# A one-core decoder layer: weight chunks taken in pairs, the later one first

## The chip, the core and the metric

The kernel runs on one core of a Trainium2 chip. The metric is the device time of one execution in microseconds (us); lower is better. Three runs of the kernel before gave a median of 2231.12 us (2229.8 to 2231.39).

## What is computed

One layer of a decoder on 256 tokens of width 2048, in float32: a gated feed-forward block (width 5504), a token mixer (two causal linear attentions, merged by gates), and a second feed-forward block, each with a norm before and one behind it.

```
f1 = swiglu(rms_norm(h, pre1), w_gate, w_up, w_down)      # (silu(x@w_gate) * (x@w_up)) @ w_down
h  = h + 0.5 * rms_norm(f1, post1)
m  = mixer(rms_norm(h, mix_pre))    # u@w_in, two attentions, gated sum of o@w_branch, then @w_out
h  = h + rms_norm(m, mix_post)
h  = h + 0.5 * rms_norm(swiglu(rms_norm(h, pre2), ...), post2)
```

## The kernel before

Every weight is read once from DRAM, in **chunks** of 128 x 1024 float32 values (512 KB). `wchunk` (L105) takes one chunk through three steps: SyncE issues a DMA into `raw` (L108), ScalarE rounds it into `whi` (L119), VectorE subtracts to get the rest, `wlo` (L120). A product is then three TensorE matmuls (`mm3`, L122): `xhi*whi` (L124), `xhi*wlo` (L125) and `xlo*whi` (L126), with the activations as the stationary operand and 512 columns of weights moving. One chunk feeds twelve such matmuls: two halves, times two token tiles, times three. `raw`, `whi` and `wlo` come from the pool `ring` with four buffers each, and each buffer is as large as the widest chunk of its tag, 2 x 528 values (4224 bytes a partition).

There are two loops over chunks. `gemm_block` (L128) makes 256 x 512 of `x @ W`: for each chunk of two k tiles it calls `mm` for token tile 0 and then 1, and then `side.pump()`, which lays one step of the small chains (transposes, attention levels) behind the twelve matmuls. It is used for the gate and up projections, for all of `w_in` and for the two branch weights. `out_proj` (L253) makes 256 x 2048 over all k tiles in eight accumulators; its chunks are one k tile by half of the columns (`hf`), in the table `order` (L278). At its first steps it also issues the products `early` on VectorE (L289), which need rows that `load_bcast` (L167) spreads over all partitions by DMA. Its last four k tiles (`tail`, L290) are used token tile by token tile; the `hf` 1 chunks of it lie in `held` buffers outside of the ring.

The order on each engine is the order of the code, as far as a scheduler keeps it: an instruction on ScalarE or VectorE that waits holds up what is behind it on that engine. At the end of a gate block ScalarE makes `silu` (L385) of both token tiles, at the end of an up block VectorE makes `hn` (L371); the down projection's left operand is split by L119 and L120 as well (`hkhi`, `hklo`). The lines that the loops consist of:

```
for k0 in range(0, nkt, 2):            # L149, gemm_block
    parts = chunk(k0, ring_alloc)
    for t in range(NT):
        mm(t, k0, parts)
    side.pump()
for i, (kt, hf) in enumerate(order):   # L280, out_proj
    parts = load(kt, hf)
    for t in range(NT):
        for n in (2 * hf, 2 * hf + 1):
            mm(t, n, kt, parts)
```

Of the kernel before, what the change touches and what calls it, by code (L numbers as in the profile page):

```python
# [16 lines left out]
D = 2048  # L17
NT = 2
# [13 lines left out]
class Side:  # L32
    """Chains of small steps whose instructions are laid between those of the large products.

    A light chain takes one step at every pump, the heavy ones take turns; a chain yields
    where the tensor engine would have to wait for what the other engines were just given."""

# [13 lines left out]
    def pump(self):  # L51
        for g in list(self.light):
            self._step(self.light, g)
        if self.heavy:
            g = self.heavy.pop(0)
            # two at a time take turns
            self.heavy.insert(min(1, len(self.heavy)), g)
            self._step(self.heavy, g)
# [12 lines left out]
def kernel(ctx: ExitStack, tc: tile.TileContext, a: dict, out: bass.AP):  # L71
# [26 lines left out]

    # ------------------------------------------------------------------ weights
    def ring_alloc(w):  # L100
# [4 lines left out]
    def wchunk(src: bass.AP, w: int, alloc=ring_alloc):  # L105
        """src: [128, 2, w] of a weight in DRAM -> the float32r parts (hi, lo) of its two halves."""
        raw = ring.tile([P, 2, w], F32, tag="raw", name=nm("raw"))
        nc.sync.dma_start(raw, src)  # L108
        parts = alloc(w)
        if len(parts) == 1:  # L110
            split_into(*parts[0], raw)
            hi, lo = parts[0]
            return [(hi[:, i, :], lo[:, i, :]) for i in range(2)]
        for i, (hi, lo) in enumerate(parts):
            split_into(hi, lo, raw[:, i, :])
        return parts
# [11 lines left out]
    def gemm_block(w_dram, c0, w, lhs, nkt=KT, held=None):  # L128
        """[256, w] of x @ W, one bank a token tile (two halves in two banks if w > 512). With
        held, the chunks after the ring's stay in its tiles, and token tile 1 comes after all  # L130
        of token tile 0."""
        nb = -(-w // CB)
        pss = [[ps_tile(f"mm{t}") for _ in range(nb)] for t in range(NT)]

        def chunk(k0, alloc):
            return wchunk(w_dram[k0 * P:(k0 + 2) * P, c0:c0 + w].rearrange("(k p) c -> p k c", p=P),
                          w, alloc)

        def mm(t, k0, parts):
            for i, part in enumerate(parts):  # L140
                kt = k0 + i
                x = lhs(t, kt)
                for j, ps in enumerate(pss[t]):
                    sl = slice(j * (w // nb), (j + 1) * (w // nb))
                    mm3(ps[:, :w // nb], x, (part[0][:, sl], part[1][:, sl]),
                        kt == 0, kt == nkt - 1)

        if held is None:
            for k0 in range(0, nkt, 2):  # L149
                parts = chunk(k0, ring_alloc)  # L150
                for t in range(NT):
                    mm(t, k0, parts)
                side.pump()
        else:
            kept = []
            for i, k0 in enumerate(range(0, nkt, 2)):
                kept.append((k0, chunk(k0, ring_alloc if i < 4 else held)))
                mm(0, *kept[-1])
                side.pump()
            for k in kept:  # L160
                mm(1, *k)
                side.pump()
            side.flush()
        return pss if nb > 1 else [ps[0] for ps in pss]

    # ------------------------------------------------------------------ helpers
    def load_bcast(name, after):  # L167
        """A row of 2048 on every partition, in four tiles; not before `after` is issued."""
        ts = []
# [7 lines left out]
    def rstd(ss, n, width, tag):  # L177
        """(ss / n + eps) ** -0.5 for ss [128, width]."""
        v = small.tile([P, width], F32, tag=f"{tag}v", name=nm("v"))
# [17 lines left out]
    def lhs_of(x):  # L197
        def lhs(t, kt):
            # the products are laid behind the transposes that they read
            side.until(lambda: x[2][t] > kt)  # L200
            return x[0][t][:, kt, :], x[1][t][:, kt, :]
        return lhs

    def to_T(x, t, n, src):
        """src [128 tokens, 512] -> k tiles 4n.. of x's token tile t."""
        ps = ps_tile()
# [5 lines left out]
    def rstd4(ss, scale, tag):  # L212
        """rstd of rows of D whose squares' sums are in the four columns of ss; all but the
        last column is added up beforehand. scale: a power of two, into the result."""
        c = 1.0 / (D * scale * scale)
# [14 lines left out]
    def first_norm(t, x, rs, wcol):  # L230
        """x's token tile t = (h * w) transposed, the weights one channel a partition."""
        if t:
# [20 lines left out]
    def out_proj(w_dram, nkt, lhs, post, scale, pre, held, after):  # L253
        """acc = lhs @ W [256, 2048]; h += scale * rmsnorm(acc) * post; then the next
        sublayer's transposed operand (h * pre, and the rows' rstd, applied later), or the
        kernel's output."""
        acc = [[None] * 4 for _ in range(NT)]
        wpost = load_bcast(post, after)
        early, nxt, rs = [], None, [None, None]
        if pre is not None:  # L260
            # h * pre + rstd * acc * (post * pre): all but the second product ahead of time
            wpre = load_bcast(pre, after)
# [17 lines left out]
        for i, (kt, hf) in enumerate(order):  # L280
            parts = load(kt, hf)
            for t in range(NT):
                for n in (2 * hf, 2 * hf + 1):
                    mm(t, n, kt, parts)
            if i == 1:
# [12 lines left out]
        def finish(t, ss):  # L298
# [6 lines left out]
            if pre is None:  # L305
                # GpSimd takes one of the four
                for n in range(4):
# [46 lines left out]

    # ------------------------------------------------------------------ FFN
    def ffn(pre, x, rs, post, pre_next):
# [49 lines left out]

    # ------------------------------------------------------------------ mixer
    def mixer(x, rs):
        xl = lhs_of(x)
        w_in = a["w_in"]  # L410
        with ExitStack() as mctx:
# [11 lines left out]

            # masks of the small levels' pairs, four heads wide, and of the diagonal
            diag = mp.tile([P, P], U8, name="diag")
# [8 lines left out]

            # lower bounds of the HGRN forget gates: softmax over the two rows of logits,
            # one head a column
            lg = blk("lg")
# [34 lines left out]
            def transposed(src, dst):  # L472
                """A step later, dst = src with each 128 columns transposed."""
                yield
# [21 lines left out]
            def spawn_T(srcs, s):  # L496
                """Transposes of the two token tiles' blocks, a step later."""
                dsts = []
# [5 lines left out]
            def attention(t, qT, kT, fT, vs, gates, dv, br, b0):  # L504
                """Four heads of 128 key channels on token tile t; fT: the decays. kT holds
                each key times the decays after it in its block, qT each query times those up
                to it; from level to level the blocks double, and the pairs of a block's halves
                get their scores, as products of two factors in [0, 1]."""
                sc = blk("sc")
# [11 lines left out]
                for lv, c in enumerate(LEVELS):  # L521
# [11 lines left out]
                    else:  # L533
                        # the blocks' rectangles lie on the engine's own borders
                        for r0 in range(0, P, 2 * c):
# [99 lines left out]
            def gla_decays(code, fT):  # L635
                """exp(logsigmoid(code @ w + b) / 16), transposed; logsigmoid(y) as
                min(y, 0) - ln(1 + exp(-|y|))."""
                cs = blk("code")
# [38 lines left out]
            def hgrn_gates(y, t, g, fT, kT):  # L677
                """f = lb + (1 - lb) sigmoid(y) and 1 - f = (1 - lb) sigmoid(-y), transposed."""
                yield
# [11 lines left out]

            # ---- GLA
            qT = spawn_T([scaled(q[t], rq[t], "q") for t in range(NT)], "qT")
            # the 16 columns of the gate's code, and beside them the first 512 of h_q
            fT, hqs = [blk("fT") for _ in range(NT)], [blk("hq") for _ in range(NT)]
# [19 lines left out]

            # ---- HGRN2, four heads at a time
            for g in range(2):
# [15 lines left out]

            # ---- gated merge
            ms = []
# [24 lines left out]

    # ------------------------------------------------------------------ the layer
    warm = const.tile([P, 1], F32, name="warm")
# [60 lines left out]
```

## Time and profile before

| | us |
|---|---|
| median of three runs | 2231.12 |
| span of the profiled execution, first to last instruction | 2230.0 |
| its own time, span and what lies around it | about 2231.1, by the median |
| TensorE matmul busy (PE) | 2203.5 |
| VectorE busy (DVE) | 1183.0 |
| ScalarE busy (ACT) | 995.1 |
| HBM read, mean | 183 GB/s over the span |

The profile names no time of the profiled execution beside its span; the median lies 1.1 us above the span, and that is taken as what lies around it. PE is the matmul, PEld the weight load that goes ahead of it on TensorE, and SP the queue that issues the weights' DMAs. Matmul durations overlap, so the pace of TensorE is read from the starts of the weight loads, of which each matmul has one: a matmul starts about when the load behind its own starts.

### The profile page before, as it was taken

What the parts mean: (1) busy time and instruction counts of PE and PEld (TensorE: products, weight loads), DVE (VectorE), ACT (ScalarE), POOL (GpSimd) and SP (SyncE); (2) the same over time, 40 slices, a digit from 0 to 9 for tenths busy, and PEclk for the clock granted to TensorE, in tenths of its full rate; (3) what the DMA queues carried; (4) which work ended last, traced back from release to release, by engine and by line L of the source; (5) the groups of instructions that cost most, each with busy time, mean ns of one, the idle gap of its engine ahead of it and who ended that gap; (6) DMA issues with size and microseconds to landing.
All of it is one profiled execution on the core that took longest, in us unless ns stands there. A gap on an engine that the chain in (4) does not pass through costs nothing.

```text
span 2230.0 us, 26331 instructions
## 1 busy us (share of the span) xinstructions
PE 2203.5 (99%) x10197; PEld 1816.2 (81%) x10197; DVE 1183.0 (53%) x1278; ACT 995.1 (45%) x1202; POOL 69.1 (3%) x106
## 2 busy tenths in 40 slices
PE   8999999999999999999999999999999999999998
PEld 6888888898888788888888888878888888898886
DVE  5544444446555744657575656465444444445554
ACT  5444444444444564444434444355444444444443
POOL 0000000000000400000000000021000000000001
PEclk9999999999999999999999999999999999999999
DMA  7666666666666556655556775555666666666664
GB/s 233 186 187 185 189 186 185 189 200 205 190 192 196 159 171 189 170 148 145 155 154 174 232 204 185 183 171 177 188 189 186 184 188 189 170 217 190 191 193 135
DMA packets 189344, 410.24 MB, mean 184 GB/s; under 512 B 13681, under 2 KB 22289, under 8 KB 189218
## 3 DMA queue, kind: packets, MB, share of 16 engines
q1 hardware_dynamic: 183712, 400.21, 60.6%
q10 hardware_dynamic: 5506, 8.34, 1.2%
q8 instruction: 80, 1.31, 0.2%
q14 instruction: 46, 0.38, 0.0%
HBM read 406.41 MB, written 2.10 MB: 183 GB/s over the span
## 4 chain that ended last, share of the span: by engine, by line
PE 64%; DVE 1%; POOL 1%; ACT 0%; issue 0%; DMA 0%; POOLq 0%; ACTq 0%
PE mm L124 16%; PE mm L126 16%; PE mm L125 16%; PE acc L125 5%; PE acc L126 5%; PE acc L124 5%; PE ps L187 1%; PE ps L531 1%; PE ps L581 0%; PE ps L538 0%; POOL h L303 0%; PE ps L515 0%; DVE tmp L295 0%; DMA raw<-in_ffn_w_down_dram 0%; POOL v L218 0%
## 5 line engine op out<-in xcount | busy, mean ns | idle before, releaser
L120 DVE TENSOR_TENSOR wlo<-raw,whi 128x1024 fp32r<-128x1024 f32 (+2 forms) x740 | 898.4, 1216 | 889.3 <-ACT whi L119 888.3
L119 ACT ACTIVATE whi<-raw 128x1024 fp32r<-128x1024 f32 (+2 forms) x740 | 777.1, 1051 | 1072.5 <-PE mm L126 800.5
L124 PE MATMUL mm<-whi,xhi 128*128 128x512 f32 (+2 forms) x2096 | 817.0, 390 | 3.6 <-ACT whi L119 3.6
L125 PE MATMUL mm<-wlo,xhi 128*128 128x512 f32 (+2 forms) x2096 | 809.6, 386 | 5.0 <-DVE wlo L120 5.0
L126 PE MATMUL mm<-whi,xlo 128*128 128x512 f32 (+2 forms) x2096 | 810.0, 386 | 0.0
L125 PEld LDWEIGHTS mm<-wlo,xhi 128*128 128x128 f32 x2096 | 394.7, 188 | 84.6 <-DVE wlo L120 6.2
L124 PEld LDWEIGHTS mm<-whi,xhi 128*128 128x128 f32 x2096 | 394.2, 188 | 83.0 <-ACT whi L119 4.0
L126 PEld LDWEIGHTS mm<-whi,xlo 128*128 128x128 f32 x2096 | 394.0, 188 | 81.1 <-DVE xlo L120 0.7
L125 PE MATMUL acc<-wlo,hkhi 128*128 128x512 f32 x656 | 257.6, 393 | 0.3 <-DVE wlo L120 0.3
L124 PE MATMUL acc<-whi,hkhi 128*128 128x512 f32 x656 | 257.2, 393 | 0.5 <-ACT hT L376 0.5
L126 PE MATMUL acc<-whi,hklo 128*128 128x512 f32 x656 | 257.5, 393 | 0.0
L125 PEld LDWEIGHTS acc<-wlo,hkhi 128*128 128x128 f32 x656 | 123.2, 188 | 29.2 <-DVE wlo L120 1.3
L124 PEld LDWEIGHTS acc<-whi,hkhi 128*128 128x128 f32 x656 | 123.2, 188 | 28.7 <-ACT hT L376 1.0
L126 PEld LDWEIGHTS acc<-whi,hklo 128*128 128x128 f32 x656 | 123.1, 188 | 27.7
L217 POOL TENSOR_TENSOR v<-ss 128x1 f32<-128x1 f32 x12 | 6.3, 524 | 1691.7 <-ACT sq L228 1690.8
L124 PE MATMUL mm<-whi,oT 128*128 128x512 f32 x128 | 51.3, 401 | 0.0
L126 PE MATMUL mm<-whi,oT 128*128 128x512 f32 x128 | 50.7, 396 | 0.0
L125 PE MATMUL mm<-wlo,oT 128*128 128x512 f32 x128 | 50.6, 395 | 0.0
L119 ACT ACTIVATE hkhi<-hT 128x512 fp32r<-128x512 f32 (+1 forms) x44 | 26.9, 621 | 52.2 <-PE acc L125 52.1
L120 DVE TENSOR_TENSOR hklo<-hT,hkhi 128x512 fp32r<-128x512 f32 (+1 forms) x44 | 29.6, 679 | 31.0 <-ACT hkhi L119 31.0
L125 PE MATMUL acc<-wlo,xhi 128*128 128x512 f32 x112 | 44.1, 394 | 0.0
L126 PE MATMUL acc<-whi,xlo 128*128 128x512 f32 x112 | 44.0, 393 | 0.0
(196 smaller groups left out, 1145.0 us busy)
## 6 DMA issues: line engine op xcount, KB each, us to landing
raw<-in_ffn_w_down_dram SPq DMA_DIRECT2D x172, 512.0 KB, 4.5
raw<-in_w_in_dram SPq DMA_DIRECT2D x168, 512.0 KB, 3.8
raw<-in_ffn_w_gate_dram SPq DMA_DIRECT2D x160, 512.0 KB, 3.8
raw<-in_ffn_w_up_dram SPq DMA_DIRECT2D x160, 512.0 KB, 3.6
raw<-in_w_out_dram SPq DMA_DIRECT2D x32, 512.0 KB, 4.1
raw<-in_w_branch_gla_dram SPq DMA_DIRECT2D x16, 512.0 KB, 3.6
raw<-in_w_branch_hgrn_dram SPq DMA_DIRECT2D x16, 512.0 KB, 3.8
raw<-in_ffn_w_gate_dram SPq DMA_DIRECT2D x16, 384.0 KB, 3.3
```

The lines of the kernel that those rows point to most:

```text
L119: nc.scalar.activation(hi, src, AF.Copy)
L120: nc.vector.tensor_tensor(lo, src, hi.bitcast(F32), op=ALU.subtract)
L124: nc.tensor.matmul(ps, lhsT=xhi, rhs=whi, start=start, stop=False)
L125: nc.tensor.matmul(ps, lhsT=xhi, rhs=wlo, start=False, stop=False)
L126: nc.tensor.matmul(ps, lhsT=xlo, rhs=whi, start=False, stop=stop)
L187: nc.tensor.transpose(dst_ps[:, i * P:(i + 1) * P], src[:, i * P:(i + 1) * P], ident)
L217: nc.gpsimd.tensor_tensor(v[:, 0:1], ss[:, 0:1], ss[:, 1:2], op=ALU.add)
L531: nc.tensor.matmul(ps[:, i * 64:(i + 1) * 64], lhsT=kT[:, sl], rhs=halves(qT[:, sl])[1], start=True, stop=True)
```

## The change

In `gemm_block`, two chunks are loaded together (A, then B), and each token tile takes four k tiles in the order B's first, A's first, A's second, B's second; `pump` follows each token tile, so again twelve matmuls. In `out_proj`, from the fifth chunk on, the chunks (kt, 0) and (kt, 1) are loaded together, and (kt, 1) is multiplied first. `held` blocks and the tail stay as they are. Comments were taken out too, so lines are about ten further down behind L290.

```
+        def one(t, kt, part, start, stop):
+            x = lhs(t, kt)
+            for j, ps in enumerate(pss[t]):
+                sl = slice(j * (w // nb), (j + 1) * (w // nb))
+                mm3(ps[:, :w // nb], x, (part[0][:, sl], part[1][:, sl]), start, stop)
...
-            for k0 in range(0, nkt, 2):
-                parts = chunk(k0, ring_alloc)
-                for t in range(NT):
-                    mm(t, k0, parts)
-                side.pump()
+            for k0 in range(0, nkt, 4):
+                parts = chunk(k0, ring_alloc) + chunk(k0 + 2, ring_alloc)
+                for t in range(NT):
+                    for i, o in enumerate((2, 0, 1, 3)):
+                        one(t, k0 + o, parts[o], k0 + i == 0, k0 + i == nkt - 1)
+                    side.pump()
...
-            parts = load(kt, hf)
-            for t in range(NT):
-                for n in (2 * hf, 2 * hf + 1):
-                    mm(t, n, kt, parts)
+            if i < 4:
+                use = [(hf, load(kt, hf))]
+            elif hf == 0:
+                use = [(0, load(kt, 0)), (1, load(kt, 1))][::-1]
+            else:
+                use = []
+            for j, parts in use:
+                for t in range(NT):
+                    for n in (2 * j, 2 * j + 1):
+                        mm(t, n, kt, parts)
```

TensorE in a gate block of the first feed-forward, before: the name's last number tells chunks apart, `Activation_49` counts ScalarE's instructions and `DVE_49` VectorE's. Token tile 0 writes `mm_213`, tile 1 `mm_214`.

```order
L124 MATMUL mm_213_1148<-whi_1218,xhi_2_99 128x512 [waits Activation_49]
L125 MATMUL mm_213_1148<-wlo_1219,xhi_2_99 128x512 [waits DVE_49]
L126 MATMUL mm_213_1148<-whi_1218,xlo_4_101 128x512
...
L124 MATMUL mm_214_1149<-whi_1218,xhi_3_100 128x512
...
L124 MATMUL mm_213_1148<-whi_1236,xhi_2_99 128x512 [waits Activation_49]
L125 MATMUL mm_213_1148<-wlo_1237,xhi_2_99 128x512 [waits DVE_49]
```

The same place now:

```order
L124 MATMUL mm_213_1148<-whi_1242,xhi_2_99 128x512 [waits Activation_49]
L125 MATMUL mm_213_1148<-wlo_1243,xhi_2_99 128x512 [waits DVE_49]
L126 MATMUL mm_213_1148<-whi_1242,xlo_4_101 128x512
L124 MATMUL mm_213_1148<-whi_1236,xhi_2_99 128x512
...
L124 MATMUL mm_213_1148<-whi_1242,xhi_2_99 128x512
...
L124 MATMUL mm_214_1149<-whi_1242,xhi_3_100 128x512
...
L124 MATMUL mm_214_1149<-whi_1236,xhi_3_100 128x512
...
L124 MATMUL mm_213_1148<-whi_1278,xhi_2_99 128x512 [waits Activation_49]
```

The two waits come every 24 matmuls instead of every 12, and the moving buffer changes after 3, 9, 15 and 21 of the 24. In the whole program TensorE's instructions that wait for ScalarE fall from 767 to 431.

ScalarE at the end of a gate block, before (the `silu` rows close the block, the `whi` rows are chunks of the next one):

```order
L119 ACTIVATE whi_1019<-raw_1017 128x1024 [waits DMAHW3_49,DVE_49,PE_49]
L119 ACTIVATE whi_1037<-raw_1035 128x1024 [waits DMAHW4_49,DVE_49,PE_49]
L385 ACTIVATE silu_993<-mm_154_835,r_201 128x512 [waits PE_49]
L385 ACTIVATE silu_995<-mm_155_836,r_305 128x512 [waits PE_49]
L119 ACTIVATE whi_1055<-raw_1053 128x1024 [waits DMAHW5_49,DVE_49]
```

and now:

```order
L119 ACTIVATE whi_1007<-raw_1005 128x1024 [waits DMAHW3_49,DVE_49,PE_49]
L395 ACTIVATE silu_993<-mm_154_835,r_201 128x512 [waits PE_49]
L119 ACTIVATE whi_1037<-raw_1035 128x1024 [waits DMAHW4_49,DVE_49,PE_49]
L395 ACTIVATE silu_995<-mm_155_836,r_305 128x512 [waits PE_49]
L119 ACTIVATE whi_1043<-raw_1041 128x1024 [waits DMAHW5_49,DVE_49]
```

Both `silu` still stand ahead of the second chunk of a pair, one of them now between the two chunks.

A third place is not moved, and the prediction reads the trace there: the tail of the last down projection, where each k tile's `held` chunk has its own two waits, three matmuls apart.

```order
L124 MATMUL acc_2869_14891<-held_16365,hkhi_16385 128x512 [waits Activation_49]
L125 MATMUL acc_2869_14891<-held_16366,hkhi_16385 128x512 [waits DVE_49]
L126 MATMUL acc_2869_14891<-held_16365,hklo_16386 128x512
L124 MATMUL acc_2869_14891<-held_16371,hkhi_16385 128x512 [waits Activation_49]
L125 MATMUL acc_2869_14891<-held_16372,hkhi_16385 128x512 [waits DVE_49]
L126 MATMUL acc_2869_14891<-held_16371,hklo_16386 128x512
L124 MATMUL acc_2869_14891<-held_16377,hkhi_16395 128x512 [waits Activation_49]
L125 MATMUL acc_2869_14891<-held_16378,hkhi_16395 128x512 [waits DVE_49]
```

Only the names' numbers differ there after the change.

## Rows read from the trace of the kernel before

**Rows 1.** The page's head: span, busy time of each engine, instructions.
```profile
span 2230.0 us, 26331 instructions
...
PE 2203.5 (99%) x10197; PEld 1816.2 (81%) x10197; DVE 1183.0 (53%) x1278; ACT 995.1 (45%) x1202; POOL 69.1 (3%) x106
...
PEclk9999999999999999999999999999999999999999
```

**Rows 2.** Waits of TensorE: who for whom, us in total, times, longest.
```profile
PE mm L125 <- DVE wlo L120: 5.0, 3, 2.0
...
PE mm L124 <- ACT whi L119: 3.6, 1, 3.6
PE acc L125 <- DVE held L120: 0.8, 1, 0.8
...
PE acc L125 <- DVE wlo L120: 0.3, 1, 0.3
```

**Rows 3.** Groups by shape: busy, mean ns of one | idle before, releasers.
```profile
L120 DVE TENSOR_TENSOR wlo<-raw,whi 128x1024 fp32r<-128x1024 f32 x700 | 857.9, 1227 | 844.7 <-ACT whi L119 844.0
...
L119 ACT ACTIVATE whi<-raw 128x1024 fp32r<-128x1024 f32 x700 | 741.5, 1060 | 1021.7 <-PE mm L126 753.4 <-PE acc L126 228.5 <-issue 13.8
...
L120 DVE TENSOR_TENSOR hklo<-hT,hkhi 128x512 fp32r<-128x512 f32 x42 | 28.7, 692 | 29.7 <-ACT hkhi L119 29.7
L371 DVE SCALAR_TENSOR_TENSOR hn<-mm,r,silu 128x512 f32<-128x512 f32 x40 | 28.3, 744 | 0.6 <-PE mm L126 0.6
L385 ACT ACTIVATE silu<-mm,r 128x512 f32<-128x512 f32 x40 | 27.6, 691 | 26.5 <-PE mm L126 23.4 <-POOL r L223 3.0
```

**Rows 4.** Timeline of weight loads, two chunks of a feed-forward block: start, us.
```profile
324.01 0.19 PEld L124 LDWEIGHTS mm<-whi,xhi 128*128 128x128 f32 x1
324.24 0.19 PEld L125 LDWEIGHTS mm<-wlo,xhi 128*128 128x128 f32 x1
...
324.93 0.19 PEld L125 LDWEIGHTS mm<-wlo,xhi 128*128 128x128 f32 x1
...
326.75 0.19 PEld L124 LDWEIGHTS mm<-whi,xhi 128*128 128x128 f32 x1
326.97 0.19 PEld L125 LDWEIGHTS mm<-wlo,xhi 128*128 128x128 f32 x1
...
329.76 0.19 PEld L125 LDWEIGHTS mm<-wlo,xhi 128*128 128x128 f32 x1
```

**Rows 5.** The same view, tail of the last down projection, waits every three.
```profile
2202.80 0.19 PEld L124 LDWEIGHTS acc<-held,hkhi 128*128 128x128 f32 x1
...
2204.16 0.19 PEld L124 LDWEIGHTS acc<-held,hkhi 128*128 128x128 f32 x1
```

**Rows 6.** The same view, same tail, another chunk every three, no waits.
```profile
2208.23 0.19 PEld L125 LDWEIGHTS acc<-wlo,hkhi 128*128 128x128 f32 x1
...
2213.09 0.19 PEld L125 LDWEIGHTS acc<-wlo,hkhi 128*128 128x128 f32 x1
```

**Rows 7.** Timeline of ACT, a feed-forward block: start, us, [idle before, releaser].
```profile
327.17 1.06 ACT L119 ACTIVATE whi<-raw 128x1024 fp32r<-128x1024 f32 x1 [1.67 <-PE mm L126]
```

**Rows 8.** Timeline of DVE behind it.
```profile
328.26 1.23 DVE L120 TENSOR_TENSOR wlo<-raw,whi 128x1024 fp32r<-128x1024 f32 x1 [1.51 <-ACT whi L119]
```

**Rows 9.** Timeline of ACT, start of the first down projection.
```profile
493.95 1.06 ACT L119 ACTIVATE whi<-raw 128x1024 fp32r<-128x1024 f32 x1 [1.77 <-DMA raw<-in_ffn_w_down_dram]
...
500.49 1.07 ACT L119 ACTIVATE whi<-raw 128x1024 fp32r<-128x1024 f32 x1 [1.20 <-DMA raw<-in_ffn_w_down_dram]
504.33 1.06 ACT L119 ACTIVATE whi<-raw 128x1024 fp32r<-128x1024 f32 x1 [2.77 <-DMA raw<-in_ffn_w_down_dram]
```

**Rows 10.** Timeline of DVE there: products ahead of time, beside the chunks.
```profile
506.37 1.29 DVE L289 TENSOR_TENSOR u<-h,row 128x512 f32<-128x512 f32 x2
507.57 1.22 DVE L120 TENSOR_TENSOR wlo<-raw,whi 128x1024 fp32r<-128x1024 f32 x1
```

**Rows 11.** The page's DMA issues: count, KB each, us to landing.
```profile
raw<-in_ffn_w_down_dram SPq DMA_DIRECT2D x172, 512.0 KB, 4.5
...
raw<-in_ffn_w_gate_dram SPq DMA_DIRECT2D x160, 512.0 KB, 3.8
```

More of the change, by code (lines that the diff above doesn't have):

```diff
@@ L137, in chunk @@
                           w, alloc)
+        def one(t, kt, part, start, stop):
[3 more added lines that the diff above has]
+                mm3(ps[:, :w // nb], x, (part[0][:, sl], part[1][:, sl]), start, stop)
         def mm(t, k0, parts):
             for i, part in enumerate(parts):
[L141 to L146, printed above, removed]
+                one(t, k0 + i, part, k0 + i == 0, k0 + i == nkt - 1)
         if held is None:
-            for k0 in range(0, nkt, 2):
-                parts = chunk(k0, ring_alloc)
+            for k0 in range(0, nkt, 4):
+                parts = chunk(k0, ring_alloc) + chunk(k0 + 2, ring_alloc)
                 for t in range(NT):
-                    mm(t, k0, parts)
-                side.pump()
+                    for i, o in enumerate((2, 0, 1, 3)):
+                        one(t, k0 + o, parts[o], k0 + i == 0, k0 + i == nkt - 1)
+                    side.pump()
         else:
```

## The prediction

> **What bounds the kernel now.** I read the page's head first: TensorE's matmuls are busy for 2203.5 of 2230.0 us, and its granted clock is 9 tenths or more in every slice, so the higher of its two levels (2.4 GHz) throughout [rows 1]. Then the waits of TensorE: for weights it stands still for 5.0 + 3.6 + 0.8 + 0.3 = 9.7 us in six places [rows 2]. So the two waits of a chunk are nearly always met before TensorE comes to them; removing half of them cannot win back standing time that isn't there. What is left is the pace of the stream itself, and that is read from the starts of the weight loads.
>
> The pace isn't even. A matmul starts with the load behind its own, so a chunk's twelve matmuls are counted from its second load to the second load of the next. One chunk takes 326.97 - 324.24 = 2.73 us, the next 329.76 - 326.97 = 2.79 us [rows 4]; all along the feed-forward they take turns like this. In the quick chunk the first three take 324.93 - 324.24 = 0.69 us, 0.230 each, and the nine behind them 2.04 us, 0.2267 each; in the lagging one the mean is 0.2325. Two readings offer themselves. The waits stand at the first two matmuls of each chunk, so they could be the cause. Or it is the buffer: the ring's buffers are 4224 bytes a partition, 16 times 256 plus 128, so that neighbours lie differently within 256 bytes and chunks take turns; the `held` tiles, 4096 bytes each, all lie alike.
>
> The tail of the last down projection tells them apart. There, with two waits every three matmuls and all weights in `held` tiles, six matmuls take 2204.16 - 2202.80 = 1.36 us, 0.2267 each: the best pace, in spite of the waits [rows 5]. Some 4 us later, without any wait but with another ring buffer every three matmuls, 21 matmuls take 2213.09 - 2208.23 = 4.86 us, 0.2314 each [rows 6]. So I take a met wait at nothing, and a change of buffer at a price.
>
> The Trainium skill (TensorE: Matmul & The Clock Gate, section Back-to-back issue gap) puts a gap of columns / 2.4 + 2.5 ns between matmuls at full clock, which is 216 ns for 512 columns. No stretch here comes below 226.7, waits or none, so the measured pace decides; if the waits were the whole excess over 216, about 0.17 us a chunk, taking away some 300 pairs of them would by that page give about 51 us.
>
> **The change, part by part.**
>
> *The waits.* TensorE's instructions that wait for ScalarE fall from 767 to 431, those that wait for VectorE from 815 to 549, some 300 pairs. Price 0 [rows 5]. What hides them is that their signals come early; the end of that cover is the third part. From the other side, if the 0.01 us that a quick chunk's first three lose (0.69 less 3 x 0.2267) were theirs, up to 0.015 with rounding, 300 pairs fewer would give 4.5 us back.
>
> *The changes of buffer.* The same matmuls meet the same buffers as often as before, but in other runs: before, a run in one kind of buffer is twelve matmuls; now it is six (B's last with B's first of the next token tile, A's two), in places three. Following the ring through the built programs, I count 365 quick runs before and 643 now, and as many lagging ones. A lagging run costs the same per matmul however long it is. A quick run pays at its start: 0.01 us by the chunk [rows 4]. The tail gives a second price: steady halves would average (0.2267 + 0.2325) / 2 = 0.2296, the 21 matmuls took 0.0018 more each, 0.038 in 3.5 quick starts (21 / 6), 0.011 each [rows 4, 6]. I take 0.012 because the two agree. 643 - 365 = 278 more starts x 0.012 = **+3.3 us**. Ends: nothing; or a quick run of six never gets going and stays at 0.2314, 6 x 0.0047 = 0.028 each, 7.8 us.
>
> *The shorter lead.* Now a chunk is ready about 2.75 us after its buffer comes free: ScalarE starts 327.17 - 326.75 = 0.42 us behind the boundary, VectorE ends at 328.26 + 1.23 = 329.49 [rows 4, 7, 8]. It is needed three chunks later, at 8.3 us, so 5.5 us are spare. With pairs, two chunks are made from the boundary on: 0.42 + 1.06 + 0.03 + 1.23 + 1.23 = 3.97 us, and the one made last is needed first, 24 matmuls or 5.52 us after the boundary [rows 3, 4]. 1.5 us are spare, and 0.7 more where the first chunk's buffer comes free three matmuls earlier. In the middle of a block that holds. At a block's end two `silu` (2 x 0.69) on ScalarE or two `hn` (2 x 0.74) on VectorE come ahead [rows 3]: 5.35 or 5.45 us, still under 5.52, the more so since token tile 0's can start half a pair earlier. The SyncE queue has the same DMAs in the same order; they now come two at a time, 1.2 us apart, but `raw` comes free a whole pair ahead, 7 us for a landing of 3.8 to 4.5 [rows 11].
>
> The cover is gone at the start of the three output projections. There the rows that are spread by DMA hold up the chunks: ScalarE waits 1.77, 1.20 and 2.77 us for `raw`, and TensorE hardly notices [rows 2, 9], since 5.5 us were spare. With 1.5 us spare, 2.77 leaves 1.3 us uncovered. VectorE has per pair two chunks, two early products and up to one `hklo`: 2.46 + 1.29 + 0.69 = 4.44 us of 5.52 [rows 3, 10], so it recovers slowly but does not fall behind. One stall of 0 to 1.3 us at each of three places: I take **+2 us** as the middle. Ends: nothing, and two such stalls at each, 3 x 2.6 = 8 us.
>
> **The sum** against the profiled execution: 2230.0 + 0 + 3.3 + 2 = 2235.3 us of span, plus the 1.1 us by which the median lies above it: **2236.4 us**, 0.24% over the median of 2231.1. About 0.2% (4.5 us) is what a measurement of this kernel can tell from no change, so the forecast lies barely past that.
>
> **Rivals.**
>
> *The waits throw the stream out of step (faster).* The lagging spell begins at a wait pair, lasts twelve matmuls and then passes off. For it: the pace switches exactly where wait pairs stand [rows 4]. Against it: the best pace with waits every three, and switching without any [rows 5, 6]. Half of about 312 lagging chunks would become quick: 156 x (2.79 - 2.72) = 10.9 us, 2220 us. It decides if pace follows waits rather than buffers. Chance 0.08. What the Trainium skill's page would give has no chance beside it, since no stretch keeps its pace.
>
> *Nothing shows.* A quick run's start costs nothing at six, and token tile 0's early finish covers the late DMAs: both terms at their lower end, 2231 us. The rows' 10 ns steps leave room for it. Chance 0.14.
>
> *The lead fails at every block's end.* 5.45 of 5.52 us is hardly a margin; one transpose's copy ahead of the pair and TensorE waits. At 44 feed-forward boundaries x 0.5 us this gives 22 us, 2253 us. For it: an instruction that waits holds up all behind it on ScalarE and VectorE. Against it: token tile 0's share runs earlier, and the buffers of the first chunk come free early. Chance 0.10.
>
> That the change does less than it says is excluded by the counts of waits.
>
> **How the numbers follow.** The forecast has the remaining 0.68, between 2232 and 2247 us as its two terms go to their ends (0 to 7.8 and 0 to 8); of that I put 0.18 below 2235.6, the 0.2% line, and 0.50 above. Faster: 0.08. Same: 0.14 + 0.18 = 0.32. Slower: 0.50 + 0.10 = 0.60. The range from 2229 to 2247 holds the forecast and the case that nothing shows, 0.82; the two outer rivals stay out.
>
> **What would show it.** Right: the waits of TensorE for `whi` and `wlo` grow by about 2 us and at the output projections' starts; in mid-block, loads come at 0.227 to 0.237 with a switch of pace every six; 24 matmuls take about 5.53 us, now 5.52. ScalarE's `whi` come in pairs, each pair's second `wlo` ends about 4 us behind the boundary. Wrong: 24 matmuls in 5.45 us or less (the waits were the cause), or a gap at each block's end (the lead fails), or lagging runs that stretch beyond the buffers.

## The result and the profile after

The changed kernel takes **2235.15 us** (median of 20 runs, 2233.53 to 2237.56), the kernel before 2232.06 (median of 20): a ratio of 1.0013, interval 1.0007 to 1.0019, so about 3.1 us slower. The forecast was 2236.4 against a median of 2231.1 known then, 5.3 us slower: the right side, and too much by 2. Each listed run's time lies 1.7 to 1.9 us above its span, so the profiled execution of the kernel before took about 2231.8 us (an estimate from that), not the 2231.1 taken above; the 5.3 us do not hang on it.

The page's head for the profiled execution of the changed kernel, to be read beside [rows 1]:

```profile
span 2233.7 us, 26326 instructions
...
PE 2207.2 (99%) x10197; PEld 1817.1 (81%) x10197; DVE 1168.4 (52%) x1278; ACT 968.4 (43%) x1200; POOL 69.9 (3%) x106
...
PEclk9999999999999999999999999999999999999999
```

The span grows by 3.7 us and TensorE's busy time by the same 3.7, at the same granted clock. The same 10197 matmuls became a little slower; TensorE does not stand still much longer. Its waits say so too [rows 2]:

```profile
PE mm L125 <- DVE wlo L120: 5.5, 3, 2.1
...
PE mm L124 <- ACT whi L119: 3.9, 1, 3.9
PE acc L125 <- DVE held L120: 1.0, 2, 0.8
```

Weights cost 10.4 us of standing. Before, it was 10.0 in seven places, not the 9.7 in six that the prediction added up; one row of that view was left out there:

```profile
PE acc L124 <- ACT held L119: 0.3, 1, 0.3
```

The groups of ScalarE and VectorE are hardly touched [rows 3] (mean ns of one behind the busy time):

```profile
L120 DVE TENSOR_TENSOR wlo<-raw,whi 128x1024 fp32r<-128x1024 f32 x700 | 839.8, 1224 | 810.1 <-ACT whi L119 809.8
...
L119 ACT ACTIVATE whi<-raw 128x1024 fp32r<-128x1024 f32 x700 | 717.4, 1055 | 939.8 <-PE mm L126 678.0 <-PE acc L126 225.1 <-issue 24.6
```

What the order does is seen in the timeline of the weight loads in a feed-forward block (start, us; a matmul starts with the load behind its own) [rows 4]:

```profile
319.56 0.19 PEld L125 LDWEIGHTS mm<-wlo,xhi 128*128 128x128 f32 x1
...
320.26 0.19 PEld L125 LDWEIGHTS mm<-wlo,xhi 128*128 128x128 f32 x1
...
320.94 0.19 PEld L125 LDWEIGHTS mm<-wlo,xhi 128*128 128x128 f32 x1
...
322.33 0.19 PEld L125 LDWEIGHTS mm<-wlo,xhi 128*128 128x128 f32 x1
...
324.17 0.19 PEld L124 LDWEIGHTS mm<-whi,xhi 128*128 128x128 f32 x1
...
325.10 0.19 PEld L125 LDWEIGHTS mm<-wlo,xhi 128*128 128x128 f32 x1
```

From 319.56 to 320.94 six matmuls run in the buffer that lies like the x tile: 1.38 us, the first three of them 0.70, the other three 0.68 (0.227 each). From 320.94 to 322.33 six run in the other: 1.39. The 24 matmuls up to 325.10 take 5.54 us, where two chunks took 5.52. A quick run of six spends half its length getting up to pace.

ScalarE's timeline shows the chunks made in pairs (an x2 row is two instructions back to back) [rows 7]:

```profile
323.90 2.01 ACT L119 ACTIVATE whi<-raw 128x1024 fp32r<-128x1024 f32 x2 [3.52 <-PE mm L126]
```

and VectorE's what follows [rows 8]:

```profile
325.00 2.36 DVE L120 TENSOR_TENSOR wlo<-raw,whi 128x1024 fp32r<-128x1024 f32 x2 [3.17 <-ACT whi L119]
```

The new pair's matmuls begin with the load at 324.17. The second `wlo` of the pair after it is ready at 327.36, 3.2 us behind that, and needed 5.54 behind it: in mid-block the lead holds.

The one large new gap stands in the gate blocks of `w_in`, where VectorE already makes early products of `w_out`'s projection: the scheduler has put them that far forward, here as in the kernel before. VectorE's rows there:

```profile
1266.63 0.69 DVE L299 TENSOR_TENSOR u<-h,row 128x512 f32<-128x512 f32 x1 [2.83 <-DMA row<-in_ffn_pre_norm_dram]
1267.23 2.35 DVE L120 TENSOR_TENSOR wlo<-raw,whi 128x1024 fp32r<-128x1024 f32 x2
```

TensorE's loads behind it, by the same view:

```profile
1267.56 0.19 PEld L124 LDWEIGHTS mm<-whi,xhi 128*128 128x128 f32 x1
1269.64 0.19 PEld L125 LDWEIGHTS mm<-wlo,xhi 128*128 128x128 f32 x1 [1.90 <-DVE wlo L120]
```

`w_out`'s projection itself begins 132 us later:

```profile
1399.79 0.19 PEld L124 LDWEIGHTS acc<-whi,xhi 128*128 128x128 f32 x1
```

An early product `u` waits 2.83 us for a row that a DMA spreads, both `wlo` of the next pair stand behind it on VectorE, and TensorE's next load comes 2.08 us after the last instead of 0.23. In the kernel before, the products there waited little, and single chunks stood between them:

```profile
1263.26 0.69 DVE L289 TENSOR_TENSOR u<-h,row 128x512 f32<-128x512 f32 x1 [0.35 <-DMA row<-in_ffn_pre_norm_dram]
1263.87 1.22 DVE L120 TENSOR_TENSOR wlo<-raw,whi 128x1024 fp32r<-128x1024 f32 x1
...
1266.29 0.69 DVE L289 TENSOR_TENSOR u<-h,row 128x512 f32<-128x512 f32 x1 [0.60 <-DMA row<-in_ffn_pre_norm_dram]
```

### The profile page after: what moved, and what is told of

Its sections match the earlier page's. It is cut to its first block, busy times and chain, and to the rows that moved or that the text cites. A ratio compares the mean times of both kernels' runs of the same rounds, so it can differ in the third digit from the quotient of the medians.

```text
span 2233.7 us, 26326 instructions
## 1 busy us (share of the span) xinstructions
PE 2207.2 (99%) x10197; PEld 1817.1 (81%) x10197; DVE 1168.4 (52%) x1278; ACT 968.4 (43%) x1200; POOL 69.9 (3%) x106
## 4 chain that ended last, share of the span: by engine, by line
PE 63%; DVE 1%; ACT 1%; POOL 1%; DMA 0%; issue 0%; ACTq 0%; POOLq 0%; DVEq 0%
PE mm L124 16%; PE mm L126 15%; PE mm L125 15%; PE acc L125 4%; PE acc L126 4%; PE acc L124 4%; PE ps L541 1%; PE ps L190 1%; PE ps L591 0%; PE ps L548 0%; DVE wlo L120 0%; POOL h L313 0%; DMA raw<-in_w_out_dram 0%; PE ps L525 0%; ACT whi L119 0%
## 5 line engine op out<-in xcount | busy, mean ns | idle before, releaser
L120 DVE TENSOR_TENSOR wlo<-raw,whi 128x1024 fp32r<-128x1024 f32 (+2 forms) x740 | 878.9, 1213 | 850.4 <-ACT whi L119 850.1
L119 ACT ACTIVATE whi<-raw 128x1024 fp32r<-128x1024 f32 (+2 forms) x740 | 751.2, 1045 | 985.4 <-PE mm L126 718.4
L381 DVE SCALAR_TENSOR_TENSOR hn<-mm,r,silu 128x512 f32<-128x512 f32 (+1 forms) x44 | 32.5, 739 | 42.9 <-PE mm L126 42.6
L395 ACT ACTIVATE silu<-mm,r 128x512 f32<-128x512 f32 (+1 forms) x44 | 29.6, 673 | 35.8 <-PE mm L126 32.7
```

The lines of the kernel that those rows point to most:

```text
L119: nc.scalar.activation(hi, src, AF.Copy)
L120: nc.vector.tensor_tensor(lo, src, hi.bitcast(F32), op=ALU.subtract)
L381: nc.vector.scalar_tensor_tensor(hn[:, :w], u[:, :w], rs[t], s[:, :w], op0=ALU.mult, op1=ALU.mult)
L395: after = nc.scalar.activation(st[:, :w], g[t][:, :w], AF.Silu, scale=rs[t])
```

## The experiments

Three theories stood for the 3 us. *Buffers*: matmuls whose weights and x tile lie alike within 256 bytes are quick, the others lag, and the order cuts the quick runs up; a met wait is free. *Lead*: all of it is standing, since a pair must be ready sooner. *Waits*: the waits have a price of their own.

To tell them apart I split each profiled execution in two. The starts of consecutive weight loads give the mean time of a matmul, apart for those that lie alike and those that don't (by the addresses of the built program); times their counts (4104 and 4584 of the 8688 that are 512 wide) this is the **pace**. All intervals above 0.3 us, less 0.232 each, are the **gaps**. Times of runs are against the kernel before on the same chip.

```
kernel                  quick runs  alike ns  apart ns  pace us  gaps us  span us  median vs before
before                     365       228.05    232.47   2001.6    23.9    2230.0
changed                    643       229.18    232.02   2004.1    25.3    2233.7    +3.1
1 plain order              493       228.67    232.25   2003.1    24.7    2232.4    +4.9
1 plain order, again       493       228.72    232.20   2003.0    26.8    2234.4    +5.0
2 whole chunks             275       227.96    232.60   2001.8    28.4    2234.8    +2.3
3 projections alone        261       227.94    232.56   2001.5    26.2    2232.3    -0.9
4 blocks alone             597       229.00    232.08   2003.6    24.4    2232.5    +1.4
5 aligned, before          all       226.90      -      1971.3    25.6    2201.9   -28.0
6 aligned, changed         all       226.90      -      1971.3    32.5    2209.3   -21.2
7 apart                  192 only    227.44    232.42   2018.3    24.2    2247.9   +17.4
8 changed, repeated        643       229.19    232.05   2004.3    22.2    2230.9    +2.0
9 aligned, changed, 528    all       226.91      -      1971.4    29.0    2205.3   -27.9
10 = 9, repeated           all       226.89      -      1971.2    25.3    2201.6   -27.7
11 = 5, repeated           all       226.91      -      1971.4    27.8    2204.2   -28.6
```

Pace and gaps together give every span's difference to within 1 us (changed less before: 2.5 + 1.4 = 3.9, span 3.7). "All" is one stretch without a change of pace; "192 only" counts matmuls.

**1. Plain order.** Shorter runs than before, but nearly the waits of before:

```
-                    for i, o in enumerate((2, 0, 1, 3)):
+                    for i, o in enumerate((0, 1, 2, 3)):
```

> The change, but in a block the four k tiles of a pair are taken in the order 0, 1, 2, 3 instead of 2, 0, 1, 3; so TensorE again waits chunk by chunk (688 of its instructions wait for ScalarE and 774 for VectorE, against 431 and 549 in the change), while the chunks are still loaded by pairs. Quick runs (stretches of matmuls whose weights and x tile lie alike within 256 bytes): 493, against 365 before and 643 in the change. Theory of buffers (each quick run pays about 0.012 us at its start, a met wait nothing): 128 x 0.012 = 1.5 us over the kernel before, plus 0 to 1.5 us of standing: +1.5 to +3. Theory of waits (a wait pair costs 0.015 us, as the upper end of the prediction had it): about 250 pairs more than the change, 3.8 us more than it: about +7 over the kernel before. Theory of lead (only standing time counts): the second chunk is needed later here, so no more standing than before: 0 to +0.5.

Measured 2237.67 us (ratio 1.0025, 1.0015 to 1.0035), +4.9: more than the theory of buffers allowed, and the theory of waits asked for +7. The pace decides: +1.5 us, just what 128 more quick starts were to cost, at 688 waits for ScalarE. The rest is not pace. But the profiled execution was the fastest of the eight and shows only 0.8 us more of gaps, so the kernel was run once more for another profile.

> The first experiment's kernel again (order 0, 1, 2, 3, loaded by pairs). Its median lay 4.9 us over the kernel before, its profiled execution, the fastest of its runs, only 2.4; its matmuls' pace accounts for 1.5. Theory of lead: the rest is standing that differs from run to run, so an ordinary execution (2237 to 2241) shows 3 to 6 us more of gaps between loads than the 24.7 us of the first look, at the same mean pace (228.7 and 232.3 ns). Theory of waits: gaps as in the first look, and the matmuls themselves slower by 0.3 to 0.6 ns.

Measured 2237.2 us (1.0013 to 1.0034). The second execution has the first one's pace to 0.1 us and 2.1 us more of gaps, and its span is 2.0 longer; I had asked for 3 to 6. VectorE's rows just ahead of the first output projection show a source. In the first of the two executions:

```profile
497.26 0.69 DVE L299 TENSOR_TENSOR u<-h,row 128x512 f32<-128x512 f32 x1 [1.55 <-DMA row<-in_mix_pre_norm_dram]
497.87 0.95 DVE L120 TENSOR_TENSOR wlo<-raw,whi 128x768 fp32r<-128x768 f32 x1
```

and in the second:

```profile
498.55 0.69 DVE L299 TENSOR_TENSOR u<-h,row 128x512 f32<-128x512 f32 x1 [2.17 <-DMA row<-in_mix_pre_norm_dram]
499.16 0.95 DVE L120 TENSOR_TENSOR wlo<-raw,whi 128x768 fp32r<-128x768 f32 x1
```

The same product waits for the same row, 0.6 us longer in the second, and `wlo` comes behind it each time. TensorE stands there; its loads in the first execution:

```profile
496.36 0.19 PEld L124 LDWEIGHTS mm<-whi,xhi 128*128 128x128 f32 x1
498.87 0.19 PEld L125 LDWEIGHTS mm<-wlo,xhi 128*128 128x128 f32 x1 [2.32 <-DVE wlo L120]
```

Beyond a usual interval the gap is 2.3 us in the first execution and 2.9 in the second; in the kernel before and in the changed kernel no gap at this place is over 0.2. With the 1.5 of pace this would be most of the 4.9 us, but other gaps of the kernel before are missing here, so that sum is not shown, and how the other runs reach 2240 us stays open.

**2. Whole chunks.** The waits of the change, without short runs:

```
-                for t in range(NT):
-                    for i, o in enumerate((2, 0, 1, 3)):
-                        one(t, k0 + o, parts[o], ...)
-                    side.pump()
+                for b in (2, 0):
+                    for t in range(NT):
+                        for i in range(2):
+                            one(t, k0 + b + i, parts[b + i], ...)
+                    side.pump()
```

> The change, but in a block the later chunk of a pair is used whole, by both token tiles (12 matmuls), then the earlier one: 431 and 548 waits as in the change, 275 quick runs (162 of 12 matmuls, 81 of 24), fewer than the 365 before. Theory of buffers: 90 starts fewer than before x 0.012 = -1.1 us, plus the standing that the change has, about 1.5 us: -1 to +0.5 over the kernel before, 3 us under the change. Theory of waits: half of the pairs gone as in the change, whatever that costs or gives: the change's own time, +3. Theory of lead: the later chunk is needed first as in the change, so the change's time, +3, if that was all standing.

Measured 2235.09 us (ratio 1.0014, 1.0005 to 1.0023), +2.3: a miss for the theory of buffers as I had put it. The pace is as before (+0.2; the 90 starts fewer gave nothing back), so most of the +2.3 should be standing; the profiled execution, 1.5 us above the median of its eleven, has 4.6 us more of gaps. Its waits:

```profile
PE mm L125 <- DVE wlo L120: 8.1, 6, 2.1
...
PE mm L124 <- ACT whi L119: 4.3, 2, 3.6
```

Against [rows 2], `wlo` holds TensorE up six times instead of three. Here the buffer that is filled first comes free only at the pair's end, in the change three matmuls earlier, so the shorter lead may be the cause. That is not shown: numbers 9 and 10 below have the same order as each other, and six such waits in one execution and three in the other.

**3 and 4. One half of the change alone.** In 3 `gemm_block` is as before, in 4 `out_proj` (the diff shown with the change, one half of it taken back).

> The change in the output projections alone; the blocks are as before: 685 and 732 waits, 261 quick runs (24 matmuls long in place of 12 in the projections). Theory of buffers: 104 starts fewer x 0.012 = -1.2 us, plus the standing at the starts of the projections, 2 to 3 us (the gaps of 2.1 and 0.7 us in the trace of the change): +0.5 to +2 over the kernel before. Theory of lead: +2 to +3, all of the change. Theory of waits: less than 0.

Measured 2231.87 us (ratio 0.9996, 0.9987 to 1.0005), -0.9: no cost that can be told from none. The sign is the one that the theory of waits gave, but the pace is before's to 0.1 us although 82 waits for ScalarE are gone, so it is no evidence for a price of waits; nor did 104 quick starts fewer give anything back. The 26.2 us of gaps in the table are those of the slowest of its eleven executions.

> The change in the blocks alone; the output projections are as before: 513 and 632 waits, 597 quick runs. Theory of buffers: 232 starts more x 0.012 = +2.8 us over the kernel before, without gaps at the starts of the projections: +2 to +3. Theory of lead (all of the change's loss is standing at the projections): 0. Theory of waits: less than 0, since most of the waits that the change takes away stand in the blocks.

Measured 2234.24 us (ratio 1.0007, 0.9998 to 1.0016), +1.4, below the expected 2 to 3; pace +2.0 for 232 more starts, gaps +0.6 in the profiled execution. Nearly all of the change's pace is lost in the blocks.

**5 and 7. Where the buffers lie.** The order is that of the kernel before, except that the one block that is 528 wide loads one k tile a chunk, so that it fits a smaller buffer. In 5 the ring's buffers become 4096 bytes, so that all matmuls lie alike:

```
-        hi = ring.tile([P, 2, w], F32R, tag="whi", ...)
+        hi = ring.tile([P, 2 if w <= CB else 1, w], F32R, tag="whi", ...)
...
-        sq = work.tile([P, CB], BF16, tag="sq", ...)
+        sq = work.tile([P, CB + 64], BF16, tag="sq", ...)[:, :CB]
...
-            diag = mp.tile([P, P], U8, name="diag")
+            diag = mp.tile([P, P + 224], U8, name="diag")[:, :P]
```

In 7 the ring is that of 5 and the two small tiles are as before, but one of the two `xlo` tiles is 128 bytes longer, so that what lies behind it moves and 8496 of the 8688 lie apart.

> The kernel before, with buffers moved only: the ring's buffers are 4096 instead of 4224 bytes a partition (the one block that is 528 wide loads one k tile a chunk, so that it fits), and two small tiles are made longer by 128 and 224 bytes, so that the weights and the x tile of all 8688 matmuls of the large products lie alike within 256 bytes, where 4584 of them did not before. 775 and 820 waits, as before. Theory of buffers: 4584 matmuls x 0.0058 us (0.2325 - 0.2267) = -27 us, and 320 quick starts fewer x 0.012 = -4: 2201 to 2206 us. Theory of waits (the pace is set by the pairs of waits or by something that stands in them): no change, 2232. Theory that a change of buffer, not how it lies, is what costs: no change either, since the buffers change as often.

Measured **2204.38 us** (ratio 0.9875, 0.9861 to 0.9888).

> The kernel before, with the ring's buffers shifted by 128 bytes against the x tiles in half of their places (two tiles ahead of them are made longer), so that 8496 of the 8688 large matmuls lie apart within 256 bytes instead of 4584; nothing else moves. Theory of buffers: 3912 matmuls x 0.0055 us = +21 us, about 2252. Theory of waits, and theory that a change of buffer costs by itself: no change.

Measured 2249.73 us (ratio 1.0079, 1.0066 to 1.0092). The page's head of number 5:

```profile
span 2201.9 us, 26377 instructions
...
PE 2174.9 (99%) x10197; PEld 1816.5 (82%) x10197; DVE 1184.4 (54%) x1286; ACT 995.9 (45%) x1210; POOL 69.2 (3%) x106
```

and its weight loads 24 matmuls apart, in a feed-forward block:

```profile
318.14 0.19 PEld L126 LDWEIGHTS mm<-whi,xlo 128*128 128x128 f32 x1
...
323.58 0.19 PEld L126 LDWEIGHTS mm<-whi,xlo 128*128 128x128 f32 x1
```

The same two views of number 7, first the page's head:

```profile
span 2247.9 us, 26377 instructions
...
PE 2221.0 (99%) x10197; PEld 1821.0 (81%) x10197; DVE 1183.9 (53%) x1286; ACT 995.0 (44%) x1210; POOL 69.3 (3%) x106
```

then the loads, again 24 matmuls apart:

```profile
318.01 0.19 PEld L125 LDWEIGHTS mm<-wlo,xhi 128*128 128x128 f32 x1
...
323.58 0.19 PEld L125 LDWEIGHTS mm<-wlo,xhi 128*128 128x128 f32 x1
```

5.44 us alike, 5.57 apart, with the same number of instructions, of waits and of changes of buffer. The times lie where the theory of buffers put them (2201 to 2206; about 2252) and nowhere near "no change", which the other theories gave. This is the lever of the kernel: 45 us between the two, with nothing but addresses moved. That the distance counts, and not the place of one operand alone, can be read in the kernel before: its x tiles lie at 0 within 256 bytes and the down projection's left operand at 128. `whi` at 0 took 228.1 ns against `xhi` and 232.4 against `hkhi`, `whi` at 128 took 232.5 and 228.0.

**6, 9. The order without its runs.** The changed kernel with the buffers of 5, so that the order can cut nothing up.

> The changed kernel, with its buffers moved in the same way, so that all its large matmuls lie alike: 435 and 552 waits. Theory of buffers: the whole cost of the order is gone but for the standing of 1.5 to 3 us at the starts of the output projections: that much over the kernel before with the same buffers. Theory of waits: half of the pairs gone shows now, without the runs on top: up to 4.5 us faster than the kernel before with the same buffers. Theory that a change of buffer costs by itself: 3 us slower, and no gain of either against the kernels before and after.

Measured 2211.19 us (ratio 0.9907, 0.9892 to 0.9923), 6.8 over number 5: more standing than I had expected, at the same pace. Its waits:

```profile
PE mm L125 <- DVE wlo L120: 8.9, 6, 2.2
PE mm L124 <- ACT whi L119: 5.9, 2, 3.7
```

A part was my edit's own: in the block that is 528 wide a chunk now takes a buffer for each k tile, so a pair took all four of the ring and the next could not be made meanwhile. Number 9 pairs two buffers in that block (`(1, 0)` in place of `(2, 0, 1, 3)`, two k tiles a step).

> The changed kernel with aligned buffers, as in the run before this (2211.2 us), but in the 528-wide block, whose chunks take a ring buffer for each k tile there, a pair is two buffers instead of all four. Theory of lead: the 6.8 us of standing that the earlier one had over the aligned kernel before are half this block's own (its chunks had no second set of buffers: gaps of 2.4 us and of several 0.2 us between 759 and 798 us), half the pairs' (2.15 us at 1258 us): 2206 to 2209. Theory that the order costs by something else: no change, 2211.

Measured 2205.13 us (ratio 0.9879, 0.9865 to 0.9892), 0.9 us under what was expected: that block alone made up about 6 of the 6.8 us.

**8, 10 and 11. Early products later.** Meant to take `u` out of the way of `wlo`:

```
-            if i > 3 and early:
+            if i > 7 and early:
```

> The changed kernel, with VectorE's early products of the output projections (u and row, which wait for rows spread by DMA and have the next pair's wlo behind them on VectorE) taken from the eighth step of the loop on instead of the fourth. Theory of lead: the gap of 2.08 us at 1267.6 us and the smaller ones at 508 and 1470 us are such waits, so they go: 1 to 2.5 us under the change, so about +1 over the kernel before, what is left being the quick runs' starts. Theory of buffers alone (all of the +3 is runs): no change, still +3.

> The one before, with the early products taken from the eighth step on. Theory of lead: the last gaps that the order brings go, 2 us less: 2204 to 2206, as the aligned kernel before (2204.4). Half of the pairs of waits are gone in it and no run in lagging buffers is left, so if a met wait costs anything (up to 0.015 us a pair), up to 4.5 us less show here: 2200.

> The aligned kernel before (2204.4 us), with the early products taken from the eighth step on. Theory of lead: its gaps at 493 and 501 us, 0.8 and 1.1 us, stand behind such products or beside the rows that they wait for; with the longer lead of single chunks little more than that can go: -0.5 to -2, 2202.5 to 2204. If the products are not in the way here: 2204.4.

Measured 2235.0 us (ratio 1.0010, 1.0001 to 1.0019), 2205.33 (0.9878, 0.9864 to 0.9891) and 2204.43 (0.9872, 0.9857 to 0.9887). The edit did not do what it was meant to: the scheduler that lays out the engines' instructions put them in the same order on every engine, names apart, so these are repeats of the changed kernel, of 9 and of 5. Whether the products could be taken out of the way was thus not tried. As repeats they tell three things. First, how much the standing scatters in one and the same order. VectorE in number 8, at the place of the gap at 1267 us shown above:

```profile
1264.28 0.69 DVE L299 TENSOR_TENSOR u<-h,row 128x512 f32<-128x512 f32 x1 [0.99 <-DMA row<-in_ffn_pre_norm_dram]
1264.89 2.35 DVE L120 TENSOR_TENSOR wlo<-raw,whi 128x1024 fp32r<-128x1024 f32 x2
```

`u` waited 0.99 us instead of 2.83, TensorE's gap there is 0.07 us beyond a usual interval instead of 1.85, and the gaps add up to 22.2 us instead of 25.3, less than before's. (That execution was the fastest of its eleven, so it is no mean either.) Two waits of TensorE, first in number 9, then in its repeat, number 10:

```profile
PE mm L125 <- DVE wlo L120: 8.0, 6, 2.2
...
PE mm L125 <- DVE wlo L120: 4.5, 3, 2.2
```

Second, the gap at 1267 us stands only in kernels that have the change's blocks, and not each time: beyond a usual interval TensorE stood there for 1.85, 0.18, 2.15, 0.07, 2.09 and 0.47 us in the six profiled executions with such blocks (the changed kernel, 4, 6, 8, 9, 10), and for 0.01 at most in the other eight. Third, with eight runs each, the medians are 2204.4 us for the order before and 2205.3 for the pairs, both aligned: +0.9 us, at the same pace of 226.9 ns, and less than these intervals can tell from nothing. The order costs 3.1 us with the buffers of before and about 0.9 where no run is left to cut up; the 2.2 between them is near the 2.5 that the pace lost.

## Why the prediction was right

**Step 1, a met wait costs nothing: right.** In the aligned kernels 775 and 820 waits (number 5) and 434 and 552 (number 9) go with 226.90 and 226.91 ns a matmul. The rival by which the waits throw the stream out of step falls with this, and with number 7, where the waits of before stand and all of it lags.

**Step 2, more quick runs, +3.3 us: the right mechanism, 0.8 too much.** The pace lost 2.5 us. The step took a start at 0.012 us and "a lagging run costs the same per matmul however long it is". The rows show two larger terms that partly cancel. The quick matmuls rose from 228.05 to 229.18 ns, 4104 x 1.13 = 4.6 us, more than 3.3: in rows of six, half of a quick run is its start. But the lagging ones fell from 232.47 to 232.02, 4584 x 0.45 = 2.1 us back. That is the half-sentence that failed: a lagging run of six averages 231.6 ns, one of twelve 232.4. Net 2.5 / 278 = 0.009 us for each added run; numbers 4 and 1 give 0.009 and 0.012 (2.0 / 232 and 1.5 / 128). In the other direction the rule does not hold: numbers 2 and 3 had 90 and 104 starts fewer and gained nothing.

**Step 3, the shorter lead, +2 us: too large, in another place and for another reason.** Of the 3.1 us, 2.5 are pace, so about 0.6 is left for standing; the aligned pair gives 0.9, the profiled execution 1.4. The step saw three stalls, one at each output projection, from `raw` that comes late for ScalarE [rows 9]. There the loads stand no longer than before: 0.6 us of gaps instead of 1.6 at the first projection, 0.2 in both kernels at the second, none at the third. The rows show one large stall, 132 us ahead of the second projection, and it was VectorE that stood, waiting for a spread row in front of `u`, with the pair's `wlo` behind it, where [rows 10] show such a product in front of a single chunk. It comes and goes with the row's arrival: 1.85 us beyond a usual interval in one execution and 0.07 in another of the same order. That the lead of mid-block is enough was right: 3.2 us of 5.54, the 3.97 less the 0.7 that token tile 0's early finish gives.

**The sum and the chances.** That the total fell on the right side comes from step 2; the stalls that step 3 counted did not happen, and what stood in their place is too small and too changeable to confirm it. Of the chances, 0.60 stood on more than 0.2% slower and 0.32 on less than that either way. The 0.13% measured is of the second kind, and 20 runs of each kernel were needed to tell it from nothing.

**The rivals.** "Nothing shows" falls to the interval, 1.0007 to 1.0019; it was not far off, since the projections alone show nothing. "The lead fails at every block's end" falls: no gap of that kind stands at the 44 boundaries. Of the signs that the prediction named, the switch of pace every six, 5.53 us for 24 matmuls (5.54) and the pairs of `whi` came; the growth of the waits by about 2 us at all three projections did not: TensorE's waits for weights grew by 0.4 us in all.

## What to carry to other kernels

Where one engine is busy for 99% and its waits are met, removing met waits gained nothing here; look at the pace of its own instructions, and at what differs between stretches of unlike pace. Here that was the address of the moving weights against the stationary tile, worth 28 us (1.25%, 1.12 to 1.39) when all agree, against the 3 us that the order moved. And an edit that makes things in larger batches spends lead: it costs nothing until some late DMA stands in front of the batch on an in-order engine, so judge it by several executions, not one.

## What was not expected of the hardware

- A 512-column matmul of these kernels took 226.9 ns where weights and left operand lie at the same place within 256 bytes (number 5) and 232.4 where nearly all lie 128 bytes apart (number 7), at the same granted clock (0.997 and 0.998). Other distances lag as well, as far as the kernels hold any (means of the intervals from 200 to 300 ns): in the kernel before, 480 matmuls lie 96, 160 or 224 bytes apart and took 233.7, 233.4 and 233.3 ns; in number 7, 96 lie 32 apart and took 233.1. Why it is so, no run shows. The Trainium skill (TensorE: Matmul & The Clock Gate, section Back-to-back issue gap) gives 216 ns for 512 columns by its formula, for a matmul by itself, and 131 in a stream. No long stretch of any run here goes below 226.9, and it is the measurement that counts.
- After a lagging run the first three quick matmuls took 231.1, 232.6 and 231.5 ns (kernel before, runs of twelve), and only from about the fourth on 227: counted by the loads, the lag outlasts its cause by three matmuls.
- The same program, in the same order, stood still for 22.2 us in one execution and 25.3 in another. Several of the changes tried here move the time by less than these 3.1 us.
